# Up-projection of a gated MLP: high and low part of the rows in one product of 512 columns instead of two of 256

## The chip, the cores and the metric

The kernel runs on one core of one Trainium2 chip. The metric is the device time of one execution in microseconds, the median of several runs. Before the change it is 438.62 us (3 runs, 438.62 to 439.71). The profile is one further execution.

## What is computed

One decoder layer on 256 tokens of width 1024, in float32: an RWKV-7 time mixing and a block-sparse attention in parallel on one normalised input, both projected and merged by gates, an output projection, and then the channel mixing, which is the part that matters here:

```python
def conv_ffn(h, w_up, conv_w, conv_b, w_down):
    u = h @ w_up                                  # (256, 1024) @ (1024, 5632)
    a, b = u[..., :D_FF], u[..., D_FF:]           # D_FF = 2816
    a = lax.conv_general_dilated(a, ...) + conv_b # causal, depthwise, width 3
    return (jax.nn.gelu(a, approximate=False) * b) @ w_down

    h2 = rms_norm(x, norm2_g[l])
    x = x + conv_ffn(h2, w_ffn_up[l], ...)
```

## The kernel before

**Precision by halves.** TensorE multiplies in a reduced float32 format (`F32R`), so each operand is split into a high part and a low remainder, and each product is made of three: high by high, low rows by high weights, and high rows by low weights. The rows of the up-projection are `hh` (high) and `hl` (low), two tiles of 128 x 8 x 256 elements: 8 blocks of 128 channels by 256 tokens. They are written by `turned` (L995 to L1007): ScalarE writes `hh[:, k]` from a transposed block in PSUM (L1004) and VectorE writes `hl[:, k]` as the difference (L1005). The same two names and places are used earlier in the kernel for the input projection (`norm_t`, L313 to L363). The row scale of the norm is applied after the product, from the tile `rsb`, which `token_scale` (L1021) makes.

**Weights.** They come in tiles of 128 x 1024 elements, 512 KB each: `load_next` (L229) issues the DMA on SP's queue into one of 4 `raw` buffers, `split_hi` (L239) has ScalarE write `whi` (L246, 4 buffers) and `split_lo` (L251) has VectorE write `wlo` (L256, 3 buffers) and ask for the next load. `weights` (L261) hands out the next finished pair and emits the following splits.

**Up-projection.** For each of 11 passes j (L1048), `proj2` (L430) is called twice, once for 256 columns of a and once for 256 of b. It takes one PSUM bank (`acc`, L65: 128 x 512 elements, 3 banks in turn) and runs `wst` (L275): for each of two weight tiles (4 channel blocks each) and each half m of 128 output columns it issues 8 products of 256 columns, alternating `hh` (L284) and `hl` (L286) with the same weights, and then 4 with `wlo` and `hh` (L289). Each product has its own weight load. The two halves m lie side by side in the bank. `wst` also serves the input projection, the gates and the branch projections.

**After each result.** The a result is multiplied by the row scale into `an` (L1058, VectorE, 512 elements), goes through the convolution (L1065 ScalarE, L1067 and L1069 VectorE) and the GELU (L1071 ScalarE, tile `cv`). The b result multiplies `cv` (L1076), and `hb` gets the high (L1077) and low part (L1078) of that.

**Down-projection.** `down` (L1035) is called one pass late: after pass j has its `hb`, the 24 products of pass j-1 run (L1043 to L1045, 512 columns each, into four banks of their own that collect over all passes). So there is none between passes 0 and 1, and after the last pass there are two. The last one is written out at L1082 to L1100, with the final sum and the stores.

**Order.** The engines run in the order in which a scheduler has placed the instructions when the kernel was built: by the order of the program, but with those whose inputs are ready going ahead of those that wait. `issue_after` blocks add an order by hand, here in pass 0 behind the transposes (L1051).

Of the kernel before, what the change touches and what calls it, by code (L numbers as in the profile page):

```python
# [18 lines left out]
S = 256  # L19
# [17 lines left out]
def body(tc, x, positions, norm1_g, w_in, rwkv_mu, w_decay_up, decay_bias, w_aaa_up,  # L37
# [3 lines left out]
    act, dve, pool, pe = nc.scalar, nc.vector, nc.gpsimd, nc.tensor  # L41
    ctx = ExitStack()
    with ctx:
        cst = ctx.enter_context(tc.tile_pool(name="cst", bufs=1))
# [23 lines left out]
        def chp(name="ch"):  # L68
            return ps.tile([128, 512], F32, name=name, tag="ch", bufs=3)
# [106 lines left out]
        def col(i):  # L176
            return par[:, i:i + 1]
# [73 lines left out]
        def split_lo():  # L251
            if halves:
                raw, hi, k, c = halves.pop(0)
                n = k * c
                lo = wp.tile([128, 1024], F32R, name="wlo", tag="wlo", bufs=NLO)
                dve.tensor_tensor(lo[:, :n], raw[:, :n], hi[:, :n].bitcast(F32), op=OP.subtract)  # L256
                ready.append((hi[:, :n].rearrange("p (k c) -> p k c", k=k),
                              lo[:, :n].rearrange("p (k c) -> p k c", k=k)))
                load_next()

        def weights(n=1):  # L261

            w = ready.pop(0)
            for _ in range(n):
                split_lo()
                split_hi()
            return w
# [45 lines left out]
        def norm_t(src, g0, tagn, cuts):  # L313

            ss = sb.tile([128, 2, 4], F32, name="ss" + tagn)
            rs = sb.tile([128, 2], F32, name="rs" + tagn)
            hh = cst.tile([128, 8, S], F32R, name="hh", tag="hh")
            hl = cst.tile([128, 8, S], F32R, name="hl", tag="hl")
            xn = {(t, hf): b2("xn" + tagn, [128, 512]) for t in range(2) for hf in range(2)}
            np_ = len(cuts) - 1  # L320

            def part(t, i):

                c0, c1 = cuts[i], cuts[i + 1]
                sv = ss[:, t, i:i + 1]
                act.activation(xn[t, c0 // 512][:, c0 % 512:c0 % 512 + c1 - c0], src[t][:, c0:c1], AF.Square,
                               accum_out=sv)
                if i < np_ - 1:
                    dve.tensor_scalar(sv, sv, 1.0 / D, ss[:, t, i - 1:i] if i else NORM_EPS,
                                      op0=OP.mult, op1=OP.add)  # L330

            def first(t):
                act.activation(rs[:, t:t + 1], ss[:, t, np_ - 1:np_], AF.Sqrt, scale=1.0 / D,
                               bias=ss[:, t, np_ - 2:np_ - 1])
                dve.reciprocal(rs[:, t:t + 1], rs[:, t:t + 1])
                last = dve.tensor_scalar(xn[t, 0], src[t][:, 0:512], rs[:, t:t + 1], None, op0=OP.mult)
                if t:
                    act.activation(xn[t, 1], src[t][:, 512:1024], AF.Copy, scale=rs[:, t:t + 1])
                else:
                    last = dve.tensor_scalar(xn[t, 1], src[t][:, 512:1024], rs[:, t:t + 1], None,  # L340
                                             op0=OP.mult)
                return last.ins

            pts = []

            def turn(t):
                for j in range(4):
                    if t == 0:
                        pts.append((chp if j < 3 else atp)("xt").rearrange("p (k t c) -> p k t c", k=2, t=2))
                    for i in range(2):  # L350
                        k = 2 * j + i
                        pe.transpose(pts[j][:, i, t], xn[t, k // 4][:, k % 4 * 128:k % 4 * 128 + 128], ident)

            def second(mid=lambda a, d: None):
                for k in range(8):
                    pk = pts[k // 2][:, k % 2].rearrange("p t c -> p (t c)")
                    a = act.activation(hh[:, k], pk, AF.Copy, scale=col(g0 + k)).ins  # L357
                    d = dve.scalar_tensor_tensor(hl[:, k], pk, col(g0 + k), hh[:, k].bitcast(F32),  # L358
                                                 op0=OP.mult, op1=OP.subtract).ins
# [38 lines left out]
        hh, hl, xn, part, first, turn, second = norm_t(x_sb, G1, "1", (0, 512, 1024))  # L398
# [43 lines left out]
        with tc.issue_after(mid[0]):  # L442
            p = now(proj2())
# [5 lines left out]
        p = acc()  # L449
# [536 lines left out]


        mh, ml = mhl
        hh = cst.tile([128, 8, S], F32R, name="hh", tag="hh")
        hl = cst.tile([128, 8, S], F32R, name="hl", tag="hl")  # L990
# [18 lines left out]
        for i, (c0, c1) in enumerate(zip(WCUT, WCUT[1:])):  # L1009
            cs = slice(c0, c1)  # L1010
            ps_ = [acc()[:, 0:c1 - c0] for _ in range(2)]
# [20 lines left out]
            act.copy(rsb, p[:, 0:S])  # L1032


        def down(j, hb):  # L1035
            for i in range(2):
                wh, wl = weights()
                st = j == 0 and i == 0
                for f in range(4):
                    t, hf = divmod(f, 2)  # L1040
                    ts = slice(t * 128, t * 128 + 128)
                    cs = slice(hf * 512, hf * 512 + 512)
                    pe.matmul(fin[f], hb[:, 0, i, ts], wh[:, 0, cs], start=st, stop=False)  # L1043
                    pe.matmul(fin[f], hb[:, 1, i, ts], wh[:, 0, cs], start=False, stop=False)  # L1044
                    pe.matmul(fin[f], hb[:, 0, i, ts], wl[:, 0, cs], start=False, stop=False)  # L1045

        prev = []
        for j in range(11):  # L1048
            hb = b4("hb", (128, 2, 2, 256), F32R)
            if j == 0:  # L1050
                with tc.issue_after(mid[0]), tc.issue_after(mid[1]):  # L1051
                    pa = now(proj2())
                    token_scale()
                fin = [chp("f0"), chp("f1"), chp("f2"), atp("f3")]
            else:
                pa = now(proj2())
            an = b2("an", [128, 2, 256])
            dve.tensor_tensor(an, pa.rearrange("p (m s) -> p m s", m=2),  # L1058
                              rsb[:, None, :].to_broadcast([128, 2, S]), op=OP.mult)
            cvs = []  # L1060
            for m in range(2):
                n = 2 * j + m
                pm = an[:, m]
                cv = t1("cv")
                act.activation(cv, pm, AF.Identity, scale=cpar[:, 44 + n:45 + n],  # L1065
                               bias=cpar[:, 66 + n:67 + n])
                dve.scalar_tensor_tensor(cv[:, 1:S], pm[:, 0:S - 1], cpar[:, 22 + n:23 + n], cv[:, 1:S],  # L1067
                                         op0=OP.mult, op1=OP.add)
                dve.scalar_tensor_tensor(cv[:, 2:S], pm[:, 0:S - 2], cpar[:, n:n + 1], cv[:, 2:S],  # L1069
                                         op0=OP.mult, op1=OP.add)  # L1070
                act.activation(cv, cv, AF.Gelu)  # L1071
                cvs.append(cv)
            pb = now(proj2())
            for m in range(2):
                cv = cvs[m]
                dve.tensor_tensor(cv, cv, pb[:, m * 256:m * 256 + 256], op=OP.mult)  # L1076
                act.copy(hb[:, 0, m], cv)  # L1077
                dve.tensor_tensor(hb[:, 1, m], cv, hb[:, 0, m].bitcast(F32), op=OP.subtract)  # L1078
            prev.append((j, hb))
            if len(prev) == 2:  # L1080
                down(*prev.pop(0))
# [3 lines left out]
        for f, is_ in ((0, (0,)), (1, (0,)), (0, (1,)), (2, (0,)), (1, (1,)), (2, (1,)), (3, (0, 1))):  # L1085
# [3 lines left out]
            for i in is_:  # L1089
                wh, wl = ws[i]  # L1090
# [34 lines left out]
```

## Time and profile before

| | |
|---|---|
| median of the runs | 438.62 us |
| the profiled execution | 438.61 us, of which the span from first to last instruction is 436.8 |
| TensorE (PE) busy | 425.6 us, 97% |
| weight loads (PEld) busy | 384.0 us, 88% |
| VectorE (DVE) busy | 301.4 us, 69% |
| ScalarE (ACT) busy | 243.0 us, 56% |
| GpSimd (POOL) busy | 12.8 us, 3% |
| products, weight loads | 3600, 3600 |
| DMA | 70.76 MB, mean 162 GB/s |

Times in the rows are microseconds from the start of the span unless they are called ns. In a row of a group stand the line of the kernel, the engine, the operation, out<-in by the program's names, the shapes, the count, and behind the bars the busy time, the mean of one in ns, the idle time of the engine just before, and what ended it. PE is TensorE's products, PEld its weight loads, SPq the queue of the sync engine. In a row of a stretch stand its bounds, its length, and for each engine the busy time with the number of instructions that touch the stretch, then the granted clock of TensorE (1.00 is full), the share of the DMA engines and GB/s. The up-projections and down-projections fill the time from about 248 us to the end. A product's length covers its way through the array, and the next product starts long before it ends, so the pace of products is read from start to start.

### The profile page before, as it was taken

The numbers are of one execution on the slowest core, as the hardware profiler recorded it, in microseconds if no ns is written. First come the engines' busy times: TensorE is split into PE (matmuls) and PEld (weight loads), VectorE is DVE, ScalarE is ACT, GpSimd is POOL, SyncE is SP. The second block draws the span as 40 slices with busy tenths as digits, with TensorE's granted clock in tenths as the row PEclk, the third lists the DMA queues.
The fourth block names the chain that finished last, engine by engine and source line by source line (L and its number), as shares of the span: only waits on it lengthen the run. The fifth ranks groups of instructions, "written<-read, shape, count | busy, mean of one in ns | idle before, by whom it ended". The sixth has DMA issues, their size and how long they took to land.

```text
span 436.8 us, 8837 instructions
## 1 busy us (share of the span) xinstructions
PE 425.6 (97%) x3600; PEld 384.0 (88%) x3600; DVE 301.4 (69%) x545; ACT 243.0 (56%) x391; POOL 12.8 (3%) x21
## 2 busy tenths in 40 slices
PE   7799998999999999999999999999999999999996
PEld 3688996788899989799997899999999999999995
DVE  4695899698456568676796479576576576576573
ACT  6489852644375446777355378455455455465450
POOL 6000040000000000000000000000000000000000
PEclk9999999999999999999999999999999999999999
DMA  8764836543657331164556366655665656565612
GB/s 234 195 190 125 243 94 195 132 129 54 194 154 230 95 104 51 50 190 127 166 182 195 107 211 184 226 189 166 200 192 178 195 193 191 191 182 185 214 50 96
DMA packets 62189, 70.76 MB, mean 162 GB/s; under 512 B 8898, under 2 KB 52617, under 8 KB 62150
## 3 DMA queue, kind: packets, MB, share of 16 engines
q1 hardware_dynamic: 61750, 69.50, 53.1%
q0 software_dynamic: 400, 0.71, 0.6%
q8 instruction: 28, 0.46, 0.4%
q14 instruction: 11, 0.09, 0.1%
HBM read 68.76 MB, written 1.44 MB: 161 GB/s over the span
## 4 chain that ended last, share of the span: by engine, by line
PE 82%; DVE 5%; ACT 5%; DMA 4%; issue 1%; SPq 1%; DVEq 0%; ACTq 0%
PE acc L284 15%; PE acc L286 15%; PE acc L289 15%; PE acc L305 4%; PE f L1045 4%; PE f L1043 4%; PE f L1044 4%; PE acc L306 4%; PE acc L309 4%; DMA raw<-in_w_in_dram 4%; DVE wlo L256 2%; ACT whi L246 1%; PE ps L876 1%; PE pp L704 1%; PE py L720 1%
## 5 line engine op out<-in xcount | busy, mean ns | idle before, releaser
L246 ACT CAST whi<-raw 128x1024 fp32r<-128x1024 f32 x121 | 126.4, 1050 | 119.3 <-PE acc L286 52.6
L256 DVE TENSOR_TENSOR wlo<-raw,whi 128x1024 fp32r<-128x1024 f32 x125 | 152.2, 1219 | 53.1 <-PE acc L289 18.4
L284 PE MATMUL acc<-hh,whi 128*128 128x256 f32 x600 | 150.1, 284 | 1.7 <-ACT whi L246 0.8
L286 PE MATMUL acc<-hl,whi 128*128 128x256 f32 x600 | 148.7, 282 | 0.9 <-DVE hl L358 0.9
L284 PEld LDWEIGHTS acc<-hh,whi 128*128 128x128 f32 x600 | 113.1, 188 | 4.4 <-ACT hh L357 1.5
L286 PEld LDWEIGHTS acc<-hl,whi 128*128 128x128 f32 x600 | 113.1, 188 | 3.2 <-DVE hl L358 1.5
L289 PE MATMUL acc<-hh,wlo 128*128 128x256 f32 x600 | 95.1, 281 | 1.2 <-DVE wlo L256 1.2
L289 PEld LDWEIGHTS acc<-hh,wlo 128*128 128x128 f32 x600 | 80.9, 189 | 2.1 <-DVE wlo L256 2.0
L1044 PE MATMUL f<-whi,hb 128*128 128x512 f32 x80 | 31.1, 389 | 0.0
L1043 PE MATMUL f<-whi,hb 128*128 128x512 f32 x80 | 31.1, 389 | 0.0
L1045 PE MATMUL f<-wlo,hb 128*128 128x512 f32 x80 | 31.1, 389 | 0.0
L305 PE MATMUL acc<-whi,hh 128*128 128x512 f32 x48 | 20.2, 425 | 0.0
L306 PE MATMUL acc<-whi,hl 128*128 128x512 f32 x48 | 18.8, 393 | 0.0
L1058 DVE TENSOR_TENSOR an<-acc,rsb 128x512 f32<-128x512 f32 x11 | 7.6, 691 | 14.8 <-PE acc L289 13.9
L1045 PEld LDWEIGHTS f<-wlo,hb 128*128 128x128 f32 x80 | 15.0, 188 | 3.1
L1044 PEld LDWEIGHTS f<-whi,hb 128*128 128x128 f32 x80 | 15.0, 188 | 2.7
L1043 PEld LDWEIGHTS f<-whi,hb 128*128 128x128 f32 x80 | 15.0, 188 | 2.7
L1076 DVE TENSOR_TENSOR cv<-cv,acc 128x256 f32<-128x256 f32 x22 | 8.3, 418 | 11.5 <-PE acc L289 11.2
L309 PE MATMUL acc<-wlo,hh 128*128 128x512 f32 x48 | 15.0, 393 | 0.0
L1065 ACT ACTIVATE cv<-an,cpar 128x256 f32<-128x256 f32 x22 | 12.0, 594 | 1.4 <-DVE an L1058 0.4
L305 PE MATMUL acc<-whi,mh 128*128 128x512 f32 x32 | 12.8, 399 | 0.0
L306 PE MATMUL acc<-whi,ml 128*128 128x512 f32 x32 | 12.6, 395 | 0.0
(274 smaller groups left out, 566.1 us busy)
## 6 DMA issues: line engine op xcount, KB each, us to landing
raw<-in_w_ffn_up_dram SPq DMA_DIRECT2D x44, 512.0 KB
raw<-in_w_in_dram SPq DMA_DIRECT2D x43, 512.0 KB
raw<-in_w_ffn_down_dram SPq DMA_DIRECT2D x22, 512.0 KB
raw<-in_w_out_dram SPq DMA_DIRECT2D x8, 512.0 KB
x<-in_x_dram SPq DMA_DIRECT2D x8, 256.0 KB
raw<-in_w_branch_b_dram SPq DMA_DIRECT2D x4, 512.0 KB
raw<-in_w_branch_a_dram SPq DMA_DIRECT2D x4, 512.0 KB
out_dram<-o SPq DMA_DIRECT2D x3, 256.0 KB
```

The lines of the kernel that those rows point to most:

```text
L246: act.copy(hi[:, :k * c], raw[:, :k * c])
L256: dve.tensor_tensor(lo[:, :n], raw[:, :n], hi[:, :n].bitcast(F32), op=OP.subtract)
L284: pe.matmul(om, wh[:, k, ms], xh[:, k0 + k], start=k0 + k + m == 0, stop=False, skip_group_check=True)
L286: pe.matmul(om, wh[:, k, ms], xl[:, k0 + k], start=False, stop=False, skip_group_check=True)
L289: pe.matmul(om, wl[:, k, ms], xh[:, k0 + k], start=False, stop=k0 + k == nk - 1 and m == n - 1, skip_group_check=True)
L305: pe.matmul(ps_[t], xh[:, K, ts], wh[:, k], start=K == 0, stop=False)
L306: pe.matmul(ps_[t], xl[:, K, ts], wh[:, k], start=False, stop=False)
L309: pe.matmul(ps_[t], xh[:, K, ts], wl[:, k], start=False, stop=K == nk - 1)
L1043: pe.matmul(fin[f], hb[:, 0, i, ts], wh[:, 0, cs], start=st, stop=False)
L1044: pe.matmul(fin[f], hb[:, 1, i, ts], wh[:, 0, cs], start=False, stop=False)
L1045: pe.matmul(fin[f], hb[:, 0, i, ts], wl[:, 0, cs], start=False, stop=False)
L1065: act.activation(cv, pm, AF.Identity, scale=cpar[:, 44 + n:45 + n], bias=cpar[:, 66 + n:67 + n])
```

## The change

`hh` and `hl` become the two halves of one tile `hx`, so that for one channel block the 256 high and the 256 low values lie side by side, at both places that make them. The up-projection no longer calls `proj2` but a function `up` of its own. It takes two `acc` banks, one for each half m of the output columns. Per channel block and m it issues one product of 512 columns (high and low rows with `whi`) instead of two of 256, and then as before the product of 256 columns with `wlo` into the first half of the bank. The low rows' part collects in the second half of the bank. VectorE adds the two halves with a reduction over pairs (`summed`): for a into `an`, which is then multiplied by the row scale in place, and for b into a new tile `bs`, which multiplies `cv`.

```diff
-        hh = cst.tile([128, 8, S], F32R, name="hh", tag="hh")
-        hl = cst.tile([128, 8, S], F32R, name="hl", tag="hl")
+        hx = cst.tile([128, 8, 2, S], F32R, name="hx", tag="hx")
+        hh, hl = hx[:, :, 0], hx[:, :, 1]
...
+        def up():
+            ps_ = [acc(), acc()]
+            for k0 in (0, 4):
+                wh, wl = weights()
+                for m in range(2):
+                    ms = slice(m * 128, m * 128 + 128)
+                    for k in range(4):
+                        pe.matmul(ps_[m], wh[:, k, ms], hx[:, k0 + k].rearrange("p a s -> p (a s)"),
+                                  start=k0 + k == 0, stop=False, skip_group_check=True)
+                    for k in range(4):
+                        pe.matmul(ps_[m][:, 0:S], wl[:, k, ms], hh[:, k0 + k], start=False,
+                                  stop=k0 + k == 7, skip_group_check=True)
+            return ps_
+
+        def summed(dst, p):
+            dve.tensor_reduce(dst, p.rearrange("p (a s) -> p s a", a=2), axis=AX.X, op=OP.add)
...
-                    pa = now(proj2())
+                    pa = up()
...
-            dve.tensor_tensor(an, pa.rearrange("p (m s) -> p m s", m=2),
-                              rsb[:, None, :].to_broadcast([128, 2, S]), op=OP.mult)
+            for m in range(2):
+                summed(an[:, m], pa[m])
+            dve.tensor_tensor(an, an, rsb[:, None, :].to_broadcast([128, 2, S]), op=OP.mult)
...
-            pb = now(proj2())
+            pb = up()
             for m in range(2):
                 cv = cvs[m]
-                dve.tensor_tensor(cv, cv, pb[:, m * 256:m * 256 + 256], op=OP.mult)
+                bs = t1("bs")
+                summed(bs, pb[m])
+                dve.tensor_tensor(cv, cv, bs, op=OP.mult)
```

More of the change, by code (lines that the diff above doesn't have):

```diff
@@ L988, in body @@
         mh, ml = mhl
-        hh = cst.tile([128, 8, S], F32R, name="hh", tag="hh")
-        hl = cst.tile([128, 8, S], F32R, name="hl", tag="hl")
+        hx = cst.tile([128, 8, 2, S], F32R, name="hx", tag="hx")
+        hh, hl = hx[:, :, 0], hx[:, :, 1]
         ss = sb.tile([128, 2, 2], F32, name="ss2")
@@ L1055, in body @@
             else:
-                pa = now(proj2())
+                pa = up()
             an = b2("an", [128, 2, 256])
-            dve.tensor_tensor(an, pa.rearrange("p (m s) -> p m s", m=2),
-                              rsb[:, None, :].to_broadcast([128, 2, S]), op=OP.mult)
+            for m in range(2):
+                summed(an[:, m], pa[m])
+            dve.tensor_tensor(an, an, rsb[:, None, :].to_broadcast([128, 2, S]), op=OP.mult)
             cvs = []
```

## The prediction, on record before the result

> **What bounds the kernel now.** I read the page first: busy time, the chain that ended last, the costliest groups.
>
> ```profile
> span 436.8 us, 8837 instructions
> ...
> PE 425.6 (97%) x3600; PEld 384.0 (88%) x3600; DVE 301.4 (69%) x545; ACT 243.0 (56%) x391; POOL 12.8 (3%) x21
> ...
> PE 82%; DVE 5%; ACT 5%; DMA 4%; issue 1%; SPq 1%; DVEq 0%; ACTq 0%
> ...
> L256 DVE TENSOR_TENSOR wlo<-raw,whi 128x1024 fp32r<-128x1024 f32 x125 | 152.2, 1219 | 53.1 <-PE acc L289 18.4
> L284 PE MATMUL acc<-hh,whi 128*128 128x256 f32 x600 | 150.1, 284 | 1.7 <-ACT whi L246 0.8
> L286 PE MATMUL acc<-hl,whi 128*128 128x256 f32 x600 | 148.7, 282 | 0.9 <-DVE hl L358 0.9
> ```
>
> TensorE is busy 97% and holds 82% of the chain. The reader is to see two things more. The 284 ns of a product is its length from start to end, and products overlap, so the price must come from start to start. And the vector engine's high/low split (L256) idles for TensorE, not the reverse.
>
> So I next read the busy time by stretches, cut at the starts of products that the timeline gives, so that each stretch holds a known number of products (the counts in the rows also take in those that only reach into the stretch).
>
> ```profile
> core 0: us, PE busy (x) PEld busy (x) DVE busy (x) ACT busy (x) POOL busy (x), PEclk, DMA share, GB/s
> 209.56:212.44 2.88, 2.88 (x26) 2.88 (x25) 2.00 (x3) 1.05 (x1) 0.00 (x0) 1.00 0.54 156
> 229.92:235.52 5.60, 5.60 (x25) 4.46 (x24) 3.14 (x3) 2.11 (x3) 0.00 (x0) 1.00 0.62 191
> 257.20:271.36 14.16, 14.16 (x128) 14.16 (x126) 11.71 (x19) 11.36 (x19) 0.00 (x0) 1.00 0.75 240
> 260.48:271.36 10.88, 10.88 (x99) 10.88 (x97) 9.89 (x17) 9.56 (x16) 0.00 (x0) 1.00 0.66 202
> 276.81:288.12 11.31, 11.31 (x97) 11.30 (x96) 6.99 (x9) 6.17 (x9) 0.00 (x0) 1.00 0.57 183
> 288.12:293.56 5.44, 5.44 (x26) 4.51 (x25) 3.79 (x6) 2.54 (x5) 0.00 (x0) 1.00 0.64 201
> 276.81:422.09 145.28, 145.28 (x1057) 137.79 (x1056) 93.15 (x129) 75.87 (x105) 0.00 (x0) 1.00 0.59 185
> ```
>
> - 276.81 to 288.12 is the two up-projections of pass j=2: 96 products of 256 columns, 11.31/96 = 117.8 ns each. Weight loads fill it too (11.30).
> - 288.12 to 293.56 is one down-projection: 24 products of 512 columns, 226.7 ns each; weight loads leave gaps (4.51 of 5.44).
> - 260.48 to 271.36 is j=1: again 96 products of 256, but 113.3 ns each, exactly half of 226.7.
> - 209.56 to 212.44 is 24 products of 256 in a branch projection: 120.0 ns. 229.92 to 235.52 is 24 of 512 in the output projection: 233.3 ns.
>
> So one shape has several paces with the same granted clock, 1.00 in every row. In the regular passes, 276.81 to 422.09, TensorE never idles (145.28 of 145.28), and the waits of that part all point the other way:
>
> ```profile
> ACT whi L246 <- PE acc L286: 40.7, 28, 1.8
> ...
> DVE wlo L256 <- PE acc L289: 14.4, 9, 1.6
> DVE an L1058 <- PE acc L289: 13.9, 9, 1.5
> ```
>
> Columns are engine and line, what was waited for, total us, times, longest. VectorE is 1.5 us early at each result. Only TensorE's pace, or a new wait in front of it, can change the time there.
>
> **The change, part by part.** *Products.* Per `proj2` call, 16 pairs (hh and hl against the same weights) become 16 products of 512, and 16 products of 256 with wlo stay. Streamed columns are equal: 48 x 256 = 16 x 512 + 16 x 256 = 12288. Weight loads fall from 48 to 32. So nothing is saved in arithmetic, only whatever a 256-wide product costs above half a 512-wide one. A pass has two calls: 96 products become 32 of 512 and 32 of 256. At the paces of the regular passes that is 32 x 226.7 + 32 x 117.8 = 11.02 us against 11.31: 0.29 less, over j=2 to 10 (nine passes) 2.6 us. For j=1 it is 11.02 against 10.88, 0.14 more. j=0 has part of each pace and I count -0.1. Sum **-2.5 us**. The unknown is the pace of the new mixture. The dear end is 233.3 and 120.0 (11.31 a pass: nothing gained in nine passes, 0.4 lost in j=1, 0.2 in j=0); the cheap end 226.7 and 113.3 (10.88: 3.9 saved, and about 0.2 in j=0). I take 226.7 and 117.8, because the regular passes already switch between these two shapes, in both directions, without paying for it.
>
> The Trainium skill, "TensorE: Matmul & The Clock Gate", section "Back-to-back issue gap", gives the gap of a warm product as N/2.4 + 2.5 ns, which would be 109.2 and 215.8 ns; by it a pair saves 2.5 ns, 352 pairs 0.9 us instead of my 2.5. The trace does not agree, with 113.3 to 120.0 and 226.7, and the measurement decides.
>
> *Sums.* Each pass gains four reductions from PSUM, 512 elements to 256 (`summed`, two for the a half, two for the b half). The multiply by the row scale keeps its 512 elements and now reads SBUF. No row shows a reduction over pairs that lie 256 apart in PSUM, so I bound it:
>
> ```profile
> L829 DVE TENSOR_REDUCE r<-s 128x8 f32<-128x512 f32 x4 | 2.7, 674 | 2.9 <-ACT s L827 2.9
> L885 DVE TENSOR_REDUCE mx<-sc 128x4 f32<-128x1024 f32 x2 | 2.4, 1214 | 0.0
> L1058 DVE TENSOR_TENSOR an<-acc,rsb 128x512 f32<-128x512 f32 x11 | 7.6, 691 | 14.8 <-PE acc L289 13.9 <-ACT rsb L1032 0.9
> L943 DVE TENSOR_TENSOR gt<-gt 128x512 f32<-128x512 f32 x4 | 2.7, 684 | 0.0
> L615 DVE COPY Xb<-Xb x1: 376/376/376, 100.6 to 100.6; 128x256 f32<-128x256 f32 x1
> L574 DVE TENSOR_TENSOR KB<-kp,L x2: 1211/2068/2925, 48.5 to 60.3; 64x1024 f32<-64x1024 f32 x2
> ```
>
> A reduction costs 674 ns for 512 elements and 1214 for 1024, about a ns per element; PSUM instead of SBUF adds 7 (691 against 684); the copy at L615 reads its 256 elements 16 apart and takes 376, no worse. I take 0.69 us, 0.61 as a step (below). Twice as dear is the row of 1024, 1.13 as a step; the dearest slowdown in the trace is 2925/1211 = 2.4 fold at L574, giving 1.59.
>
> The Trainium skill, "PSUM — Partial Sum Buffer", section "Specifications (TRN2)", says that PSUM has 8-byte cache lines and that a non-contiguous pattern slows matmuls significantly; carried over to this read it would make the sums dear, which is the third case below, and no row of before shows it.
>
> What these sums lie beside, in a regular pass:
>
> ```profile
> 313.39 1.23 DVE L256 TENSOR_TENSOR wlo<-raw,whi 128x1024 fp32r<-128x1024 f32 x1 [1.60 <-PE acc L289]
> 316.16 0.69 DVE L1058 TENSOR_TENSOR an<-acc,rsb 128x512 f32<-128x512 f32 x1 [1.54 <-PE acc L289]
> 316.77 1.22 DVE L256 TENSOR_TENSOR wlo<-raw,whi 128x1024 fp32r<-128x1024 f32 x1
> ...
> 319.48 1.22 DVE L256 TENSOR_TENSOR wlo<-raw,whi 128x1024 fp32r<-128x1024 f32 x1
> 321.88 0.75 DVE L1076 TENSOR_TENSOR cv<-cv,acc 128x256 f32<-128x256 f32 x2 [1.19 <-PE acc L289]
> ```
>
> The next operation starts 0.61 after L1058. VectorE's busy time per pass is 6.99 + 3.79 = 10.78 of 16.75 us; four steps make it 13.2 of the new 16.46. That is covered, and the cover ends when a step costs (16.46 - 10.78)/4 = 1.42 us. Behind the sums wait the splits L256, one per weight tile, of which three fit ahead; in these rows a split starts when a slot frees, two tiles before its use, so it may slip by about 4 us. The hb halves of a pass are used a whole pass later, and for j=10 after a down-projection of 5.44 us. Both are free.
>
> *Banks.* One call took one `acc` bank; it now takes two of the three. So the second bank of b's call is a's first. It is full 1.4 us before a's call ends (a quarter of 11.02/2) and wanted 1.4 us after. The reduction must fit in those 2.8 us, on an engine that stood idle 1.54 us just then: free in regular passes. The first two passes have no down-projection between them, and there VectorE is behind:
>
> ```profile
> 264.00:271.30 7.30, 7.30 (x67) 7.30 (x66) 7.00 (x12) 6.04 (x12) 0.00 (x0) 1.00 0.69 205
> ```
> ```profile
> 264.10 0.75 DVE L1076 TENSOR_TENSOR cv<-cv,acc 128x256 f32<-128x256 f32 x2 [0.29 <-ACT cv L1071]
> 264.77 1.22 DVE L256 TENSOR_TENSOR wlo<-raw,whi 128x1024 fp32r<-128x1024 f32 x1
> 265.90 0.75 DVE L1078 TENSOR_TENSOR hb<-cv,hb 128x256 fp32r<-128x256 f32 x2
> 266.57 0.68 DVE L1058 TENSOR_TENSOR an<-acc,rsb 128x512 f32<-128x512 f32 x1
> 267.18 1.21 DVE L256 TENSOR_TENSOR wlo<-raw,whi 128x1024 fp32r<-128x1024 f32 x1
> ```
>
> It is busy 7.00 of 7.30. j=1's first sum would run where L1058 stands, 266.57 to about 267.2, and its bank is wanted at about 267.3 (260.48 plus five eighths of 10.88). j=0's four sums, 2.4 us, come before it; the idle time of 257.20 to 271.36 is 14.16 - 11.71 = 2.45 and takes most. The wait is 0 to 2.3 us; I take **+0.5**, near the covered end.
>
> *Tile hx* is the old hh and hl side by side, same bytes, written and read in the same pieces: nothing. No DMA is added or moved; SP's and POOL's queues are unchanged.
>
> **Sum**, against the profiled execution, 438.61 us (436.8 of span and 1.8 around it), which agrees with the median 438.62: 438.61 - 2.5 + 0.5 = **436.6 us**.
>
> **Rivals.** *Wide products gain nothing.* The mixture runs as the output projection does: 32 x 233.3 + 32 x 117.8 = 11.24 a pass, 0.6 saved in nine passes, 0.4 lost in j=1, 0.1 in j=0, the wait 0.5: 439.0. For it: 113.3 is exactly half of 226.7, and pace here depends on where operands lie, which changes. Against: the same up/down alternation at 117.8 and 226.7 nine times over. By the rule of the Trainium skill cited above it would be 438.61 - 0.9 + 0.5 = 438.2.
>
> *VectorE becomes the bound.* Place: the reductions. At 1.59 a step the regular pass needs 10.78 + 6.4 = 17.1 against 16.46, 0.7 x 9 = 6.2 us; before 271.36 six reductions are 9.5 us, less 2.45 idle and 3.4 of room (the split started at 267.18 ends at 268.4, its product starts about 271.8), 3.6. Total 438.6 - 2.5 + 6.2 + 3.6 = 446. It decides from about 1.4 us a step, in the regular passes as at the start, where (2.5 + 5.9)/6 = 1.4. For it: a PSUM reading order that no row shows. Against: L615 and L829.
>
> **How the numbers follow.** The forecast's case has 0.52, its own range 434.5 (cheap end, no wait) to 437.3 or, with a long wait, 438.4; no gain 0.28 (438 to 440); VectorE bound 0.17; something faster still 0.03. Measurement tells about 0.3%, 1.3 us: faster means below 437.3, slower above 439.9. Faster 0.46 + 0.03 = 0.49; same 0.06 + 0.22 = 0.28; slower 0.06 + 0.17 = 0.23. The range reaches from 434.4 to 441.5 (dear products, +0.6, and the whole wait, +2.3) and leaves out most of the VectorE case.
>
> **What would show it.** Right: wide products of `up` 226 to 227 ns apart and the narrow ones 113 to 118; a pass of 16.4 to 16.5 us; TensorE without idle time from j=2; reductions near 0.69 us; a short wait of TensorE for a reduction, if any, before 271 us. Wrong: wide products near 233; reductions above 1.4 us; splits ending after their products could start; TensorE waiting at the second bank in every pass.

## The result, and the profile after

The changed kernel takes **437.27 us** (median of 7 runs, 436.13 to 438.07) against 438.62 us before (7 runs, 437.96 to 439.71). The ratio is 0.9967, with a 95% interval of [0.9952, 0.9982]: a third of a per cent faster, and 0.7 us slower than the 436.6 us forecast. The profiled execution took 437.27 us, 435.5 of it span.

The page of the kernel after: span, busy time, the share of the chain, and the groups that the change touches.

```profile
span 435.5 us, 8161 instructions
...
PE 424.9 (98%) x3248; PEld 367.7 (84%) x3248; DVE 327.6 (75%) x589; ACT 241.9 (56%) x391; POOL 12.8 (3%) x21
...
PE 80%; ACT 6%; DVE 6%; DMA 4%; issue 1%; SPq 1%; DVEq 0%; ACTq 0%
...
L1044 PE MATMUL acc<-hx,whi 128*128 128x512 f32 x352 | 96.7, 395 | 0.6 <-DVE bs L1052 0.6
...
L1047 PE MATMUL acc<-hx,wlo 128*128 128x256 f32 x352 | 54.6, 278 | 0.0
...
L1052 DVE TENSOR_REDUCE an<-acc 128x256 f32<-128x512 f32 x22 | 15.2, 689 | 7.2 <-PE acc L1047 6.3
```

There are 352 products and weight loads fewer, 16 us less work for the weight loads, and 26 us more for VectorE. Yet TensorE's busy time falls by only 0.7 us: almost all that the change removes was hidden, and the bound is where it was. A reduction takes 689 ns, as estimated (0.69).

The busy time of the kernel after by stretches, cut as before at the starts of products: up-projections of passes 0 and 1, from the last transposes (L1001) in front of them; a down-projection; the two up-projections of pass 2; all from there to the last down-projections; the rest. Columns as in the prediction.

```profile
core 0: us, PE busy (x) PEld busy (x) DVE busy (x) ACT busy (x) POOL busy (x), PEclk, DMA share, GB/s
247.39:271.68 24.29, 23.73 (x139) 20.25 (x138) 21.65 (x36) 16.93 (x28) 0.00 (x0) 1.00 0.48 153
271.68:277.14 5.46, 5.46 (x27) 4.51 (x25) 4.99 (x11) 3.37 (x7) 0.00 (x0) 1.00 0.66 200
277.14:288.24 11.10, 11.10 (x65) 9.68 (x64) 8.94 (x11) 5.37 (x7) 0.00 (x0) 1.00 0.74 233
277.14:420.72 143.58, 143.58 (x769) 123.27 (x768) 114.35 (x163) 74.49 (x103) 0.00 (x0) 1.00 0.61 190
420.72:435.50 14.78, 11.06 (x50) 8.83 (x48) 8.15 (x15) 2.27 (x5) 0.00 (x0) 1.00 0.20 72
```

The same cuts of the kernel before, where the prediction has not shown them:

```profile
247.69:271.36 23.67, 23.45 (x204) 23.18 (x202) 19.18 (x32) 18.09 (x31) 0.00 (x0) 1.00 0.55 176
...
422.09:436.83 14.74, 11.04 (x50) 8.83 (x48) 6.84 (x11) 1.47 (x3) 0.00 (x0) 1.00 0.20 71
```

From these the difference of the two spans adds up:

| stretch | before | after | difference |
|---|---|---|---|
| up to the last transposes in front of the up-projections | 247.69 | 247.39 | -0.30 |
| passes 0 and 1, to the first down-projection | 23.67 | 24.29 | +0.62 |
| nine periods, first to last down-projection (271.36 to 422.09; 271.68 to 420.72) | 150.73 | 149.04 | -1.69 |
| the last two down-projections and the stores | 14.74 | 14.78 | +0.04 |
| span | 436.83 | 435.50 | -1.33 |

The first line isn't the change's: among the kernels below this stretch ended anywhere from about 247 to 249 us. The change made a regular pass 0.19 us shorter (16.56 for 16.75) and the start 0.62 longer. In the regular passes TensorE has no idle time at all, 143.58 of 143.58 us, so the gain there is a matter of pace alone.

One block of eight products of pass 2 in the timeline after (start, length, and how many):

```profile
282.70 1.09 PE L1044 MATMUL acc<-hx,whi 128*128 128x512 f32 x4
283.62 0.62 PE L1047 MATMUL acc<-hx,wlo 128*128 128x256 f32 x4
284.08 0.39 PE L1044 MATMUL acc<-hx,whi 128*128 128x512 f32 x1
```

Four wide products take 0.92 us from first start to the next line's, four narrow ones 0.46. The starts in the trace are finer: the wide ones stand 226, 236, 231 and 236 ns apart (233 or 234 in the block that follows a down-projection), the narrow ones 118, 114, 113 and 113. So a wide product costs 232.4 and a narrow one 114.5: 32 x 232.4 + 32 x 114.5 = 11.10, the row of the stretch. The forecast had 226.7 and 117.8.

And the one wait that was added, in the waits after (what was waited for, total us, times, longest) and in VectorE's timeline:

```profile
PEld acc L1044 <- DVE bs L1052: 1.0, 1, 1.0
PE acc L1044 <- DVE bs L1052: 0.6, 1, 0.6
```
```profile
260.34 0.98 DVE L1087 SCALAR_TENSOR_TENSOR cv<-an,cpar,cv 128x255 f32<-128x255 f32 x2 [0.74 <-ACT cv L1085]
261.23 0.88 DVE L1089 SCALAR_TENSOR_TENSOR cv<-an,cpar,cv 128x254 f32<-128x254 f32 x2
262.02 1.28 DVE L1052 TENSOR_REDUCE bs<-acc 128x256 f32<-128x512 f32 x2
```

Once, at 261.8 us, TensorE stands: the second bank of a's call in pass 1 is the first bank of b's call in pass 0, and that bank is summed only at 262.02, because the convolution (L1087, L1089) is queued ahead of the sum on VectorE and itself waited 0.74 us for ScalarE.

### The profile page after: what moved, and what is told of

The parts are those of the page before. It is cut to its first block, busy times and chain, and to the rows that moved or that the text cites. A ratio compares the mean times of both kernels' runs of the same rounds, so it can differ in the third digit from the quotient of the medians.

```text
span 435.5 us, 8161 instructions
## 1 busy us (share of the span) xinstructions
PE 424.9 (98%) x3248; PEld 367.7 (84%) x3248; DVE 327.6 (75%) x589; ACT 241.9 (56%) x391; POOL 12.8 (3%) x21
## 4 chain that ended last, share of the span: by engine, by line
PE 80%; ACT 6%; DVE 6%; DMA 4%; issue 1%; SPq 1%; DVEq 0%; ACTq 0%
PE acc L1044 17%; PE acc L1047 8%; PE acc L284 6%; PE acc L286 5%; PE acc L289 5%; PE acc L305 4%; PE f L1063 4%; PE f L1062 4%; PE f L1064 4%; PE acc L306 4%; PE acc L309 4%; DMA raw<-in_w_in_dram 3%; DVE wlo L256 2%; ACT whi L246 2%; PE ps L876 1%
## 5 line engine op out<-in xcount | busy, mean ns | idle before, releaser
L1044 PE MATMUL acc<-hx,whi 128*128 128x512 f32 x352 | 96.7, 395 | 0.6 <-DVE bs L1052 0.6
L1044 PEld LDWEIGHTS acc<-hx,whi 128*128 128x128 f32 x352 | 60.1, 188 | 9.1 <-DVE bs L1052 1.0
L284 PE MATMUL acc<-hx,whi 128*128 128x256 f32 x248 | 64.0, 292 | 0.7 <-ACT whi L246 0.5
L286 PE MATMUL acc<-hx,whi 128*128 128x256 f32 x248 | 62.5, 285 | 0.3 <-DVE hx L358 0.2
L1047 PEld LDWEIGHTS acc<-hx,wlo 128*128 128x128 f32 x352 | 53.4, 188 | 7.9
L1047 PE MATMUL acc<-hx,wlo 128*128 128x256 f32 x352 | 54.6, 278 | 0.0
L284 PEld LDWEIGHTS acc<-hx,whi 128*128 128x128 f32 x248 | 47.4, 191 | 2.9 <-ACT whi L246 0.7
L286 PEld LDWEIGHTS acc<-hx,whi 128*128 128x128 f32 x248 | 47.4, 191 | 1.9 <-DVE hx L358 0.7
L289 PE MATMUL acc<-hx,wlo 128*128 128x256 f32 x248 | 40.1, 285 | 1.0 <-DVE wlo L256 0.9
L289 PEld LDWEIGHTS acc<-hx,wlo 128*128 128x128 f32 x248 | 33.8, 192 | 1.7 <-DVE wlo L256 1.6
L1052 DVE TENSOR_REDUCE an<-acc 128x256 f32<-128x512 f32 x22 | 15.2, 689 | 7.2 <-PE acc L1047 6.3
L305 PE MATMUL acc<-whi,hx 128*128 128x512 f32 x48 | 20.3, 425 | 0.0
L306 PE MATMUL acc<-whi,hx 128*128 128x512 f32 x48 | 18.8, 392 | 0.0
L309 PE MATMUL acc<-wlo,hx 128*128 128x512 f32 x48 | 15.0, 393 | 0.0
```

Source lines behind the costliest of these rows:

```text
L284: pe.matmul(om, wh[:, k, ms], xh[:, k0 + k], start=k0 + k + m == 0, stop=False, skip_group_check=True)
L286: pe.matmul(om, wh[:, k, ms], xl[:, k0 + k], start=False, stop=False, skip_group_check=True)
L289: pe.matmul(om, wl[:, k, ms], xh[:, k0 + k], start=False, stop=k0 + k == nk - 1 and m == n - 1, skip_group_check=True)
L305: pe.matmul(ps_[t], xh[:, K, ts], wh[:, k], start=K == 0, stop=False)
L306: pe.matmul(ps_[t], xl[:, K, ts], wh[:, k], start=False, stop=False)
L1044: pe.matmul(ps_[m], wh[:, k, ms], hx[:, k0 + k].rearrange("p a s -> p (a s)"), start=k0 + k == 0, stop=False, skip_group_check=True)
```

## Experiments

Each kernel ran beside runs of the kernel before on the same chip; the heading gives the median of before there. Kernels under one heading ran on one chip, except e8_pace and e9_place.

### The parts alone: layout, sums, no sums, longer blocks (before: 438.72 us)

**e1_layout**, the kernel before with the tile `hx` alone:

```diff
-            hh = cst.tile([128, 8, S], F32R, name="hh", tag="hh")
-            hl = cst.tile([128, 8, S], F32R, name="hl", tag="hl")
+            hx = cst.tile([128, 8, 2, S], F32R, name="hx", tag="hx")
+            hh, hl = hx[:, :, 0], hx[:, :, 1]
```

> Only the tile hx of the change: high and low rows side by side, and the products, banks and sums of before. If the layout alone moved nothing: a regular pass of 16.75 us with narrow products 117.8 ns apart, time 438.6 us as before. If it is the place of the rows that sets the pace of the narrow products: 113.3 ns, a pass of 16.34, and about 434.7 us.

Measured: 439.05 us, ratio 1.0 [0.9983, 1.0017], regular pass 16.75 us, products 117.8 ns apart. The layout moves nothing there. Passes 0 and 1 took longer than before, though:

```profile
248.13:272.33 24.20, 23.97 (x203) 23.70 (x202) 19.26 (x32) 18.02 (x31) 0.00 (x0) 1.00 0.53 174
```

That is 24.20 us for the 23.67 of before: the same 96 narrow products of pass 1 ran 117.8 ns apart here and 113.3 in the profile of before. The layout doesn't decide it, since e5_first below has the same layout and the same passes 0 and 1 and took 23.67 again. In each case the row begins behind the same two small transposes (those of `token_scale`); what decides its pace there stays open.

**e2_sums**, the changed kernel, but each wide product taken apart again into two narrow ones (into the two halves of the bank). The banks, the sums and the layout stay:

```diff
-                        pe.matmul(ps_[m], wh[:, k, ms], hx[:, k0 + k].rearrange("p a s -> p (a s)"),
-                                  start=k0 + k == 0, stop=False, skip_group_check=True)
+                        pe.matmul(ps_[m][:, 0:S], wh[:, k, ms], hh[:, k0 + k], start=k0 + k == 0, stop=False, ...)
+                        pe.matmul(ps_[m][:, S:], wh[:, k, ms], hl[:, k0 + k], start=False, stop=False, ...)
```

> The change without its wide products: hh and hl are multiplied in two products of 256 into the two halves of two banks, and VectorE adds the halves. Theory (the gain is the products' alone, the sums cost only the wait at the start): narrow products 117.8 ns apart, a regular pass of 16.75 us, TensorE waiting 0.5 to 1 us before 271 us, 439.2 us. Rival (the sums or the second bank cost time in every pass): a pass above 16.8 us and TensorE idle in it, 440 us or more.

Measured: 439.67 us, ratio 1.0018 [1.0001, 1.0035]. A regular pass is 16.75 us as before, and the only new gap is this one:

```profile
263.11 0.28 PE L1044 MATMUL acc<-hx,whi 128*128 128x256 f32 x1
264.01 0.39 PE L1044 MATMUL acc<-hx,whi 128*128 128x256 f32 x1 [0.63 <-DVE bs L1054]
```

Here 0.90 us pass from start to start, where 0.12 is usual, and the median is 0.95 above that of before. Sums and banks therefore cost about 0.9 us in all, once, at the same bank as in the changed kernel, and nothing in the regular passes. What the changed kernel gains there comes from the wide products.

**e3_nosums**, the changed kernel without the sums. It uses the first half of each bank only and so leaves the low rows' part out of the result:

```diff
-                summed(an[:, m], pa[m])
-            dve.tensor_tensor(an, an, rsb[:, None, :].to_broadcast([128, 2, S]), op=OP.mult)
+                dve.tensor_tensor(an[:, m], pa[m][:, 0:S], rsb, op=OP.mult)
...
-                summed(bs, pb[m])
-                dve.tensor_tensor(cv, cv, bs, op=OP.mult)
+                dve.tensor_tensor(cv, cv, pb[m][:, 0:S], op=OP.mult)
```

> The change without its sums: only the first half of each bank is used, which leaves the low rows' part out of the result. Theory: the regular pass stays at 16.56 us, because its sums lie beside TensorE's work; the wait of 0.7 us between the first two passes goes; 436.5 us. Rival (sums cost time in the regular passes too): a pass of 16.4 us or less, 435 us.

Measured: 437.87 us, ratio 0.9983 [0.9969, 0.9997]: 1.4 us above what was expected. The regular pass is 16.56 us, unchanged, as expected. But another wait took the place of the one taken away. The timeline at that place:

```profile
256.38 0.43 PE L1031 MATMUL prs<-ident,rx 128*128 128x128 f32 x2
256.85 0.37 ACT L1032 COPY rsb<-prs 128x256 f32<-128x256 f32 x1
257.25 0.76 DVE L1078 TENSOR_TENSOR an<-acc,rsb 128x256 f32<-128x256 f32 x2 [0.94 <-ACT rsb L1032]
...
257.82 0.94 PE L1044 MATMUL acc<-hx,whi 128*128 128x512 f32 x3 [1.01 <-DVE an L1078]
```

Without the sums, a's banks are emptied by the multiply with the row scale (L1078), which in pass 0 needs `rsb`, made of two transposes that stand at that point in TensorE's own order. b's second bank is a's first, so TensorE waits 1.01 us. The sum needs no `rsb` and frees the bank earlier: in pass 0 it removes one wait while it makes another. Taking the sums away therefore doesn't isolate the price of the wait; e10_spare does.

**e4_wide8**, the changed kernel with eight wide products in a row and then eight narrow ones, by a loop over m of its own for each kind.

> The change with another order: for a weight tile the 8 wide products of both halves first, then the 8 narrow ones. Theory of settling (a wide product after narrow ones is slow until about three have run, as at the start of each down-projection): distances near 226 236 231 236 and then 227 for the last four, narrow ones then 118; a pass of about 16.55 us, 437.3 us. Theory of place (wide products of these tiles run at 233 however many follow each other): all but the first near 233 to 235, narrow ones near 113; a pass of about 16.55 us too. The time is the same in both, the distances tell.

Measured: 437.17 us, ratio 0.9967 [0.9947, 0.9987], pass 16.56 us. The wide ones stand 226, 235, 231, 236, 231, 236, 231 and 235 ns apart. They do not settle at 226.7 in a longer run, so the dear wide product is no matter of a start after a change of width. Nor does the pass gain by having half as many changes of width as the changed kernel.

### Wide products used once, alternated, and the sums tripled (before: 438.73 us)

**e5_first**, the kernel before with the `hx` layout, and in a's call of passes 2 to 10 only the first block of four pairs as four wide products. All other products stay narrow and collect in one half; only the one bank with two halves is summed:

```diff
+                    for k in range(4):
+                        if k0 + m == 0:
+                            pe.matmul(ps_[m], wh[:, k, ms], hx[:, k].rearrange("p a s -> p (a s)"), ...)
+                        else:
+                            for xv in (hh, hl):
+                                pe.matmul(ps_[m][:, 0:S], wh[:, k, ms], xv[:, k0 + k], ...)
...
-                pa = now(proj2())
+                pa = up1() if j > 1 else now(proj2())
```

> Before, with one block of wide products at the start of each regular pass: in passes j=2 to 10 the first 4 pairs of a's call (first weight tile, first half of the columns) are 4 wide products into one bank, and one sum adds its halves; all else of the up-projection is narrow, the first two passes are as before. Theory of pace (narrow products run at 113.3 ns after wide ones of these tiles and at 117.8 after a down-projection, and keep the pace that they start with): first block 4 x 233.4 + 466 ns = 1.40 us, seven blocks of 1.36, a pass of 16.38 us, and 438.7 - 9 x 0.37 = 435.4 us. Rival (narrow products fall back to 117.8 by themselves): a pass of 16.73 us, 438.5 us.

Measured: **435.42 us** (434.66 to 435.49), ratio 0.9913 [0.9883, 0.9943], faster than both kernels. Its two up-projections of pass 2:

```profile
276.80:287.72 10.92, 10.92 (x94) 10.73 (x92) 7.84 (x11) 6.07 (x9) 0.00 (x0) 1.00 0.58 189
```

The four wide products take 0.93 us (233, 233, 234, 233 ns apart), the 88 narrow ones behind them the other 9.99: 113.5 each. In the kernel before, and in e1_layout from the same tiles, the same narrow products run at 117.8 behind a down-projection. So narrow products keep a pace that they got from what ran ahead of them. In the changed kernel about half of the 0.21 us that the up-projections of a pass gain is this: 32 narrow products at 114.5 for 117.8 are 0.11 us, and 32 wide ones at 232.4 for two narrow ones at 117.8 (235.6) are 0.10. Against two narrow products at 113.3 (226.6) a wide one of `hx` is the dearer, which is why one block of them gains more than all.

**e6_altern**, the changed kernel with wide and narrow products one by one in turn (one run).

> The change with wide and narrow products in turn, channel block by channel block. In the change the first wide product after a narrow one takes 226 ns and the others 231 to 236. If it is the narrow product in front that makes a wide one cheap: 226 + 113 to 118 ns a pair, a pass of 16.3 to 16.5 us, 435 to 436.8 us. If it is the change of width that costs (the step from the last wide product to the first narrow is 236, and the next 118): 236 + 118 a pair, a pass of 16.8 us, 439.5 us.

```profile
278.81:290.12 11.31, 11.31 (x66) 9.83 (x65) 8.14 (x11) 5.25 (x7) 0.00 (x0) 1.00 0.68 213
```

Measured: 440.85 us. The 32 wide and 32 narrow products take 11.31 us, as much as the 96 narrow ones of before, with wide ones about 235 and narrow ones 118 ns apart. The narrow products lose their gain: in blocks too the first one behind a wide product takes 118, and only those after it 113 or 114; here each is a first one. The premise of the prediction that the regular passes change width without paying was read from two changes in a pass. A price for each change isn't shown, since e4_wide8, with half the changes of the changed kernel, has its pass of 16.56.

**e7_sum3**, each sum done three times over (one run).

> The change with every sum done three times over. VectorE theory (the sums are free until a step costs 1.42 us): a step is now 1.83 us, VectorE needs 10.78 + 4 x 1.83 = 18.1 us a pass against 16.56, nine passes 13.9 us more, the start some 3 to 6 us more, 454 to 457 us, with TensorE waiting for splits or banks. Rival (VectorE has more room than its busy time shows, or the waits arise at once): 16.56 us a pass and 437 us, or well over 457.

Measured: 460.68 us, 3.7 above the upper end of what was expected. Two periods of the regular part, and from the waits of the whole run:

```profile
305.89:342.07 36.18, 34.40 (x177) 28.23 (x176) 35.29 (x55) 17.59 (x24) 0.00 (x0) 1.00 0.58 177
```
```profile
PE acc L1044 <- DVE bs L1053: 6.2, 6, 2.3
...
PEld acc L1047 <- DVE wlo L256: 5.2, 5, 1.0
```

A pass is 18.1 us in the mean of the two, and VectorE is busy 35.29 of 36.18: it has become the bound, and TensorE waits for sums and for splits. The prediction's arithmetic for this rival, 10.78 us of other work and a step of 0.61 for each reduction, gives 10.78 + 12 x 0.61 = 18.1. The mechanism is real; only its price was far from deciding. Its whole time is not the price of the sums alone, though: in this run the products of the down-projections stand in pieces among those of the up-projections, so TensorE's order changed too, and where the 3.7 us come from is not shown.

### The pace by itself (before: 438.73 and 438.54 us)

Both kernels are the changed one with rows of products appended at the end, whose results go nowhere, so their times (505.87 and 524.75 us, one run each) mean nothing beside the others. Before each row stands a row like the down-projection's, with a weight tile moving and `hb` stationary.

```diff
+        def line(p, st, mv, n):
+            for i in range(24):
+                pe.matmul(p[:, 0:n], st(i), mv(i), start=i == 0, stop=i == 23)
```

**e8_pace**, 24 products of a kind.

> The change with rows of 24 products added at the end, for their pace alone; between two rows stands one in the manner of the down-projection (stationary hb, moving weights, 512 wide). If the pace of wide products hangs on the moving tile: rows that move hx take 233 ns whatever is stationary, rows that move weights 227. If it hangs on the stationary tile: rows with whi stationary take 233 whatever moves, rows with hb 227. If it hangs on the data: whi stationary with zeros moving takes 227. Narrow rows behind a down-projection: 117.8.

Moving `hx` against `whi`; moving `hx` against `hb`; moving weights against `whi`; moving `hb` against `whi`; narrow, moving `hx` against `whi`:

```profile
436.93:442.53 5.60, 5.60 (x25) 4.49 (x24) 0.00 (x0) 0.00 (x0) 0.00 (x0) 1.00 0.00 0
447.99:453.59 5.60, 5.60 (x25) 4.49 (x24) 0.00 (x0) 0.00 (x0) 0.00 (x0) 1.00 0.00 0
459.05:464.49 5.44, 5.44 (x25) 4.50 (x24) 0.00 (x0) 0.00 (x0) 0.00 (x0) 1.00 0.01 3
469.93:475.37 5.44, 5.44 (x25) 4.50 (x24) 0.00 (x0) 0.00 (x0) 0.00 (x0) 1.00 0.00 0
491.69:494.52 2.83, 2.83 (x25) 2.82 (x24) 0.00 (x0) 0.00 (x0) 0.00 (x0) 1.00 0.03 6
```

Divided by 24: 233.3, 233.3, 226.7, 226.7 and 117.9 ns. Weight loads leave gaps in all the wide rows, and the clock is 1.00 in all. The wide product is dear with `hx` moving, whichever of the two is stationary. Two more rows of this run: zeros moving against `whi` took 226.7, and narrow products with weights moving against `hb` 120. The zeros lie in a tile of their own, so that row alone doesn't tell their value from their place.

**e9_place**, 16 wide or 24 narrow products, with `hx` read from other starts and from a copy.

> The change with rows of 16 to 24 products added at the end, for their pace alone, each behind a row in the manner of the down-projection. Theory of place (the pace of a wide product hangs on where its moving tile lies, not on its values): a copy of the first two channel blocks of hx in another tile runs at 226.7 ns, every piece of hx at 233.4 whatever its offset. Rival (the values, or the start within the tile): the copy runs at 233.4 too, or the pieces differ by their offset. Narrow rows of hx: 117.8 behind a down-projection row, 113.3 for all 24 behind 4 wide products of hx, and if one wide product is enough, 113.3 behind one.

Moving `hx` from its start; moving a copy of the same values in another tile; moving `hx` from 64 bytes further on; moving weights against stationary `hx`; then narrow: the copy; `hx` behind weights; `hx` behind four wide `hx`:

```profile
435.98:439.71 3.73, 3.73 (x17) 2.99 (x16) 0.00 (x0) 0.00 (x0) 0.00 (x0) 1.00 0.00 0
443.36:446.99 3.63, 3.63 (x18) 3.00 (x16) 0.00 (x0) 0.00 (x0) 0.00 (x0) 1.00 0.00 0
458.01:461.63 3.62, 3.62 (x17) 3.00 (x16) 0.00 (x0) 0.00 (x0) 0.00 (x0) 1.00 0.00 0
494.78:498.45 3.67, 3.67 (x18) 3.00 (x16) 0.00 (x0) 0.00 (x0) 0.00 (x0) 1.00 0.00 0
502.09:504.96 2.87, 2.87 (x26) 2.87 (x24) 0.00 (x0) 0.00 (x0) 0.00 (x0) 1.00 0.00 0
508.61:511.44 2.83, 2.83 (x25) 2.82 (x24) 0.00 (x0) 0.00 (x0) 0.00 (x0) 1.00 0.00 0
512.37:515.11 2.74, 2.74 (x26) 2.73 (x25) 0.00 (x0) 0.00 (x0) 0.00 (x0) 1.00 0.00 0
```

The same values cost 3.73/16 = 233 ns a product from `hx` and 3.63/16 = 227 from the copy, and `hx` itself costs 3.62/16 = 226 from a start 64 bytes further on. Starts 256, 512 or 1024 bytes further took 233 again, and one 16 bytes further 235; 233.4 had been expected of all of them, that at 64 bytes too. The copy rules out the values as the cause. A narrow product is 2.87/24 = 119.6 from the copy and 117.9 from `hx`; and behind wide products of `hx`, 114.2 in mean, 113.3 from the third on. One wide product in front did as much as four.

### The bank that waits (before: 438.54 us)

**e10_spare**, the changed kernel with b's second bank taken from the attention's banks (`at`), of which one is free by then:

```diff
-        def up():
-            ps_ = [acc(), acc()]
+        def up(spare=None):
+            ps_ = [acc(), spare() if spare else acc()]
...
-            pb = up()
+            pb = up(atp)
```

> The change with a fourth bank: the second bank of b's call is a free one of another group, so no call waits for a sum of the call before. Theory (the wait of 0.7 us between the first two passes is for a bank that the sums of b still hold): the wait goes, regular passes stay at 16.56 us, 436.5 us. Rival (VectorE is late there anyway, and the wait comes back at a split): 437.2 us.

Measured: 436.25 us (435.93 to 437.11), ratio 0.9957 [0.9943, 0.9971]. Passes 0 and 1, from the transposes in front of them:

```profile
246.96:270.35 23.39, 23.39 (x140) 20.25 (x139) 20.85 (x34) 16.93 (x28) 0.00 (x0) 1.00 0.47 150
```

TensorE has no idle time (23.39 of 23.39). The stretch is 0.90 us shorter than the 24.29 of the changed kernel, which is the price of the wait, and 0.28 shorter than the 23.67 of before, which is what the products save in passes 0 and 1 against that profile. Against the 24.20 of e1_layout it would be 0.81. The regular pass stays at 16.56.

### Moving the tile (before: 438.46 us)

**e11_shift**, the changed kernel, and **e12_shift_before**, the kernel of e1_layout, with `hx` 64 bytes further on in its buffer:

```diff
-            hx = cst.tile([128, 8, 2, S], F32R, name="hx", tag="hx")
+            hx = cst.tile([128, 16 * S + 16], F32R, name="hx", tag="hx")[:, 16:].rearrange(
+                "p (k a s) -> p k a s", k=8, a=2)
```

> The changed kernel with the one tile hx moved by 16 elements (64 bytes) in its buffer, at both places that make it; nothing else. Theory that the pace hangs on where the moving tile starts: the wide products of up go at 226.7 ns instead of 232 to 233, as in the appended row of the same shift. The narrow ones take 113 to 120. With 118 the regular pass is 32 x 226.7 + 32 x 118 + 5.44 = 16.47 us against 16.56, and the time about 436.5; with 120 it is 16.53 and about 437.0; with 113.3, 16.32 and about 435.1. Rival, that the appended rows had their pace from what ran just before them and not from the place: wide products stay at 232 to 233, the pass at 16.56, the time at 437.3.

> The kernel before with hh and hl as the halves of one tile hx (which alone moved nothing), and that tile moved by 64 bytes; all products stay 256 columns. Theory of the place: the narrow products leave their 117.8 ns. If they take the 120.0 of the appended copy, the regular pass is 96 x 120.0 + 5.44 = 16.96 us against 16.75, and the time about 438.6 + 9 x 0.21 = 440.5, plus what the earlier projections lose by the same tile. If they take 113.3, the pass is 16.32 and the time about 434.7. Rival, that place matters to wide products alone: pass 16.75, time 438.6.

Measured: 437.03 us, ratio 0.9975 [0.9957, 0.9993], and 438.56 us, ratio 1.0002 [0.9986, 1.0017]. The up-projections of pass 2, of the one and of the other:

```profile
277.44:288.55 11.11, 11.11 (x65) 9.69 (x64) 8.77 (x11) 5.40 (x7) 0.00 (x0) 1.00 0.75 235
```
```profile
276.65:287.98 11.33, 11.33 (x98) 11.30 (x96) 6.99 (x9) 6.19 (x9) 0.00 (x0) 1.00 0.60 179
```

Nothing moved: the same 226, 236, 231, 236 and 118, 113, 114, 113 in the one and 117.8 in the other. So my theory that the start of the moving tile sets the pace falls. The built programs show what the edit had done: the tile had grown by 64 bytes too, so all tiles behind it, the weights among them, moved by 64 as well. Modulo 128 bytes `hx` starts at 32 and the weight tiles and `hb` at 96, in the changed kernel as in e8_pace and e9_place (the copy of e9_place too); in e11_shift `hx` starts at 96 and the weights at 32. What stayed the same is the *distance* of the two operands.

Sorted by that distance, these rows of the case agree:

| moving, stationary | start of both, modulo 128 bytes | ns per product |
|---|---|---|
| 512: weights, `hb` (down-projection) | 96, 96 | 226.7 |
| 512: `hb`, `whi` (e8) | 96, 96 | 226.7 |
| 512: copy, `whi` (e9) | 96, 96 | 227 |
| 512: `hx` + 64 bytes, `whi` (e9) | 96, 96 | 226 |
| 512: `hx`, `whi` (e8, e9) | 32, 96 | 233 |
| 512: `hx`, `hb` (e8) | 32, 96 | 233 |
| 512: `hx` + 16 bytes, `whi` (e9) | 48, 96 | 235 |
| 512: weights, `hx` (e9: 3.67/16) | 96, 32 | 229 |
| 512: weights, `mh` (output projection) | 96, 0 | 233.3 |
| 256: `ybh`, `whi` (branch projection); copy, `whi` (e9); weights, `hb` (e8) | 96, 96 | 120.0; 119.6; 120 |
| 256: `hx` or `hh`, `whi` | 32, 96 | 117.8 or 113.3 |

With equal starts the wide product is cheapest and the narrow one dearest; with unequal starts it is the other way. This is an ordering that fits, found after the fact. The run that would test it, `hx` alone moved against the weights (16 elements in front and 16 behind), was not tried, and why a distance should matter stays open. So does why, with the same unequal starts, a row of narrow products goes at 117.8 behind a down-projection and at 113.3 behind a wide product of `hx`, and at either behind the two transposes of `token_scale` (before and e1_layout); that it does is shown by e5_first and e9_place, and by those two profiles.

## Why the prediction was right, and which terms were off

- **The bound.** Right: TensorE's pace alone decides in the regular passes, before (145.28 busy of 145.28) and after (143.58 of 143.58).
- **Products, -2.5 us.** The mis-sized term. Nine passes give -1.7 (9 x 0.19), not -2.6, and passes 0 and 1 give -0.28 against the profile of before (e10_spare), not +0.04: -2.0 in all. The step that failed is "I take 226.7 and 117.8, because the regular passes already switch between these two shapes". The 226.7 belonged to another pair of tiles (weights moving, `hb` stationary), and with `hx` moving a wide product takes 232.4. That was the rival's premise, "the mixture runs as the output projection does", and for the wide products it came true, with one of the signs listed for a wrong prediction, "wide products near 233"; the regular pass, 16.56, lies above the 16.4 to 16.5 listed for a right one. What the rival missed is that the narrow products gain: behind wide ones they take 114.5, not 117.8. Had they kept 117.8, the pass would have gained 11.31 - 32 x (232.4 + 117.8) / 1000 = 0.10 us instead of 0.21. That a gain of the forecast's order came out owes half to this, which the prediction didn't have: that part was luck.
- The Trainium skill, "TensorE: Matmul & The Clock Gate", section "Back-to-back issue gap", gives N/2.4 + 2.5 ns as the gap of an isolated product, 109.2 and 215.8 for these widths; the prediction carried it over to a stream. The trace doesn't agree: 114.5 and 232.4 here, and from 113.3 to 120.0 and from 226.7 to 233.3 elsewhere. By the rule a pair saves 2.5 ns; measured, a wide product takes 235.6 - 232.4 = 3.2 ns less than the pair, and the narrow product behind it another 3.3 less, for which the rule has no term.
- **Sums, free.** Right: 689 and 684 ns for the rows where 690 was taken, and VectorE at 114.35/143.58 x 16.56 = 13.2 us a pass, the figure forecast. e2_sums shows that the regular pass doesn't feel them; e7_sum3 that it does when VectorE needs 18.1 us a pass. The warning carried over from the Trainium skill, "PSUM — Partial Sum Buffer", section "Specifications (TRN2)", on non-contiguous patterns does not show in this read: pairs that lie 1 KB apart in PSUM cost 689 ns, where the neighbouring elements of L829, in SBUF, cost 674.
- **The wait, +0.5 us.** The mechanism and the time (before 271 us, once) right, the place not, the price 0.9 (24.29 - 23.39). I had looked at a's sum in front of b's second bank in pass 1. That bank was free in time. The one that was late is a's second bank in pass 1, held by b's sum of pass 0, because VectorE takes the convolution first. The rule that decides is in the order of an engine, not in its share of busy time.
- **Layout, nothing.** Right (e1_layout, ratio 1.0).
- **Sum.** -2.0 from the products and +0.9 from the wait are -1.1; the rest of the span's -1.33 is 0.30 of an earlier start and 0.04 lost at the end, neither of the change. The two errors have one sign: 0.5 less gained, 0.4 more waited, 0.9 in all. The time missed by only 0.7 because of the earlier start, which is luck too.

## What to carry to other kernels

A pace read from rows holds for those operands in those places, not for a shape: before costing a product that doesn't exist yet, look for a row with the same moving and the same stationary tile, and where there is none keep the whole spread as the term's range. Where one call takes more of a ring of buffers (buffers handed out in turn), list for each buffer who releases it and what stands ahead of the releaser in its engine's order, for the first passes above all; a spare buffer (e10_spare) was worth 0.9 us here. And a change that merges work can pay by what it does to its neighbours: four wide products a pass (e5_first) were worth more than thirty-two.

## What was not expected of the hardware

- One and the same narrow product (256 columns, same tiles, clock 1.00, back to back) runs at 117.8 or at 113.3 ns for a whole row, and one wide product of the same moving tile in front of the row is enough to change it: 4% of the up-projection's time. With no wide product in front, pass 1 ran at 113.3 in the profile of before and at 117.8 in that of e1_layout.
- The pace of a product depends on where its operands lie: a wide product costs 233 ns from `hx` and 227 from a copy of the same values, or from `hx` with the start moved by 64 bytes, while moving both operands by 64 bytes changed nothing.
- The version with one wide block (435.42 us, ratio 0.9913 [0.9883, 0.9943]) gains by the pace of the narrow products; its arithmetic is that of the kernel before but for one sum in each of nine passes.
